# Sixteen chunks of the first feed-forward computed with tokens on the output's partitions

## The chip, the cores and the metric

The kernel runs on one core of a Trainium2 chip. The metric is the device time of one execution in microseconds (us), the median of several runs. The engines are TensorE (PE for its matmuls, PEld for its weight loads), VectorE (DVE), ScalarE (ACT), GpSimd (POOL) and SyncE (SP), which here only issues DMAs. Each engine works through its own queue in order and waits on semaphores for the others.

## What is computed

One layer of a hybrid decoder: 512 tokens (T) of 1024 channels (D), float32 in and out. A SwiGLU feed-forward, a token mixer (recurrent heads beside attention) and a second feed-forward, each between two normalisations. The change touches the first feed-forward, with F = 2816 hidden channels, 22 chunks of 128:

```python
def rms_norm(x, g):
    xf = x.astype(jnp.float32)
    y = xf * lax.rsqrt(jnp.mean(xf * xf, axis=-1, keepdims=True) + RMS_EPS)
    return (y * g.astype(jnp.float32)).astype(x.dtype)

def swiglu(x, w_gu, w_down):
    gate, up = jnp.split(x @ w_gu, 2, axis=-1)
    return (jax.nn.silu(gate) * up) @ w_down
...
        x = x + 0.5 * rms_norm(swiglu(rms_norm(x, ffn1_pre_g[l]), ffn1_w_gu[l], ffn1_w_down[l]), ffn1_post_g[l])
...
        x = x + 0.5 * rms_norm(swiglu(rms_norm(x, ffn2_pre_g[l]), ffn2_w_gu[l], ffn2_w_down[l]), ffn2_post_g[l])
```

Of the mixer only one thing matters here: its recurrence needs a decay factor for each channel, worked out from the parameter lru_lambda alone.

## The kernel before

**Precision.** Every float32 product is done as three matmuls of reduced width: each operand is split into a rounded copy (hi, made by ACT) and the remainder (lo, made by DVE), and hi x hi, hi x lo and lo x hi are summed in PSUM. A weight tile thus costs one ACT copy ("cast") and one DVE subtraction ("low") after it is loaded.

**Seven products for eight.** Most of both feed-forwards uses the Strassen-Winograd scheme: a product of 2 x 2 blocks is made of seven block products ("forms") and sums of blocks. On the weight side the forms p to v need four sums or differences, made in place on the raw tile by DVE before the cast ("pre", run by `combine`: q, r, s and t). On the other side the forms of the normalised input (`nxt.t`) are made once. For the down product the forms of the hidden values are made by `seven_left` and `seven_right` as the values come, with some left in `hid.steps` to be run inside the down product.

**The weight stream.** `Weights` (W) holds the list of raw weight tiles (1 MB each, loaded by SP in two DMAs of 512 KB) and the list of units, that is, of hi and lo pairs made from them, in the order in which TensorE takes them. `W.take(ahead)` keeps the splitting some units ahead; a unit is cast as one ACT instruction of 128x1024, and its low as one DVE instruction of the same size. When the last unit of a raw tile is split, the next raw tile's load is issued (`W.load`), unless something else is owed at that place (`W.owed`). `W.later(n, fn)` runs fn at the n-th take from now. All instructions go out in the program's order, engine by engine (`manual_schedule`): what an engine does next is fixed by that order.

**FFN1.** `GROUPS1` divides the 22 chunks into (0, 4), (4, 8), (8, 12), (12, 16) and (16, 22).
- Group 0 is `classic`: plain products, then a plain down product (matmuls at L421 to L423) whose partial sums go to HBM. At its end `lend` stores the input x to HBM (xT_hbm) to free its buffers.
- Chunks 4 to 21 are made by `quad` (L773), nine times, two chunks at a time. The weights are stationary (128x128), 256 tokens move, and gate and up come out with channels on the partitions: 7 forms of 24 matmuls (L786) into the PSUM banks A, D and B. ACT copies A to B (L805), and ACT and DVE do the sums of the scheme, silu and the product, which gives hidden values with channels on the partitions, as the down product wants them.
- The down product of groups 4, 8 and 12 is `seven_down` with `by_channels` (L1114, matmuls L1122), straight after the group's two quads: 7 forms of 24 matmuls with 256 columns. ACT copies each result to a stage tile, and POOL adds it to the partial sums in HBM (yp_a) by accumulating DMAs (L895).
- The last group (16 to 21) has three quads and a plain down product of 8 output columns, which begins with the earlier sums coming back (`parts`, loaded by POOL's queue); `decay_factor` (L1042, 16 operations on 128x4 and one table of ACT's) runs beside it at its second column.

**FFN2** has quads too, but its `seven_down` is given `by_tokens` (L1624): there the hidden values are stationary, 512 weight columns move, and the sums have tokens on the partitions (matmuls L1630 to L1632, 84 for the seven forms). It begins by turning its input: DVE transposes 32x32 blocks (L1616) and SP puts the pieces to HBM (L1619).

Of the kernel before, what the change touches and what calls it, by code (L numbers as in the profile page):

```python
# [8 lines left out]
F32 = mybir.dt.float32  # L9
# [6 lines left out]
P = 128  # L16
T = 512
# [102 lines left out]
def tile_layer(ctx: ExitStack, tc: tile.TileContext, out: bass.AP, **ins: bass.AP):  # L120
# [94 lines left out]
    def add_quad(w_gu, f, name):  # L215
# [31 lines left out]
        unit(d, "u")  # L247
        unit(b, "v")

    def add_seven_down(wd, f, name):  # L250

        rx, ry = (W.raw(lambda i=i: load_raw([wd[0, (f + k) * P:(f + k + 2) * P, HALF_D[i]] for k in (0, 2)], 2, D, f"{name}{'yx'[i]}d{f}_")) for i in (1, 0))
        first, second = HALF_D
        b11, b21, b12, b22 = (ry, first), (ry, second), (rx, first), (rx, second)

        def of(block):
            return W.tiles[block[0]][:, :, block[1]]

        def unit(block, n, pre=None):
            def cast(raw):  # L260
                hi, lo = w_tiles(2, T, f"{name}d{n}{f}_")
                act.copy(hi, of(block))
                return hi, lo

            def low(raw, hi, lo):
                dve.tensor_sub(lo, of(block), hi.bitcast(F32))

            W.unit(block[0], cast, low, pre)

        def combine(fn, o, x, y):  # L270
            def run():
                assert max(o[0], x[0], y[0]) < W.loaded
                fn(of(o), of(x), of(y))
# [14 lines left out]
        add()  # L288
    GROUPS1 = [(0, 4), (4, 8), (8, 12), (12, 16), (16, 22)]
    for g, (f0, f1) in enumerate(GROUPS1):  # L290
        for f in range(max(f0, 2), f1, 2):
            (add_gate_up if f < CLASSIC1 else add_quad)(w1, f, "a")
        if SEVEN_DOWN1[0] <= f0 < SEVEN_DOWN1[1]:
            add_seven_down(ins["ffn1_w_down"], f0, "a")
# [408 lines left out]
    class Hidden:  # L703
# [66 lines left out]

            self.steps = [lambda: self.low("s2"), last_sum, lambda: self.low("s4"), lambda: self.low("a22")]

        def quad(self, f, last, ahead, seven_down=False):  # L773

            n = f"{self.name}{f}"
            l, r = HALF
# [28 lines left out]
            act.copy(B, A)  # L805
            seven(D, "t3", True)
            act.copy(p7, D)
            seven(A, "t2", False)
            act.copy(u2, A)
            seven(B, "b21", False)  # L810
            W.later(1, act.activation, p1, B, AF.Silu)
            seven(A, "t1", False)
            act.copy(u4, A)
            W.later(1, dve.tensor_add, u4, p7, u4)
            seven(D, "t4", False)
            dve.tensor_add(u2, u2, D)
# [10 lines left out]
            if not seven_down:  # L827
                for j in range(2):
                    self.hs[f + j] = hs[j]

        def classic(self, n, banks, extra, ahead=AHEAD):

# [44 lines left out]
    def seven_down(hid, f, one, part):  # L877


        forms = hid.seven_forms(f)  # L880
# [230 lines left out]
    def in_halves(t):  # L1111
        return t.rearrange("p (a b) -> p a b", a=2)
# [20 lines left out]
        return tiles  # L1133

    parts = [None] * KD
    late = []
    for g, (f0, f1) in enumerate(GROUPS1):
        if SEVEN_DOWN1[0] <= f0 < SEVEN_DOWN1[1]:
# [3 lines left out]
            continue  # L1142
        if f1 == FC:
            W.owed = [lambda: None, lambda: x_tiles.__setitem__(slice(None), give_back())]
        xs = hid.chunks(f0, f1) if g else hid.classic(f1, banks, {})
        if f1 == FC:
            for c in range(KD):
                parts[c] = t2k(f"yp_a{c}")
                pool.dma_start(in_halves(parts[c]), in_hbm[c // 2][:, :, c % 2])  # L1149
        for c in range(KD):  # L1150
            if f1 == FC and c == 0:
                load_gates()
                neg = masks()
            if f1 == FC and c == 1:
                ka, nka = decay_factor()
                preload(AF.Sqrt)
            if f1 == FC and c == 3:
                split_gates()
            if f1 == FC and c >= KD - LATE:
                late.append((c, W.take(0)))  # L1160
                W.fill(3)
                continue
            if c == 0:

                two = [W.take(), W.take()]
                pair_banks = [bank(f"ya{g}{i}") for i in range(2)]
                for k, x in enumerate(xs):
                    for w, b in zip(two, pair_banks):
                        mm3(b, w, k, x, k == 0, k == len(xs) - 1)
            b = pair_banks[c] if c < 2 else product(W.take(), xs, name=f"ya{g}{c}")  # L1170
            if g == 0 and c in (0, 1, 3, 4):
                (n1.sums if c in (0, 3) else n1.lows)(2 + c // 3)
            if g == 0:
                st = t2k("stage")
                act.activation(st, b, AF.Copy, scale=-1.0 if c >= KD // 2 else 1.0)
                pool.dma_start(in_hbm[c // 2][:, :, c % 2], in_halves(st))
                if c == 4:
                    lend(x_tiles)
            else:
                res.chunk(c, b, parts[c])  # L1180

# [565 lines left out]
```

## Time and profile before

| | |
|---|---|
| Time, median of 3 runs | 865.41 us (865.25 to 865.65) |
| The profiled execution's own time | 865.51 us |
| Its span, first to last instruction | 863.8 us |
| TensorE's granted clock in it | 0.998 |
| Busy: PE, PEld | 855.4 us, 797.9 us |
| Busy: DVE, ACT, POOL | 705.0 us, 522.0 us, 219.5 us |
| Moved over DMA | 125.53 MB, mean 145 GB/s |
| First quad of FFN1 starts | 78.64 us |
| First `seven_down` of FFN1 | 118.96 to 139.12 us |

A page of the profile gives busy times of each engine, their share of the span, and the chain of waits: the work that ended last, followed back from the last instruction, at each step to what released it or to the instruction before it on its engine. Lines of groups read "line engine operation output<-input, shape, xcount". Names such as raw_ax, whi_aq or wlo_aq are a raw weight tile of FFN1 and the hi and lo of its unit q; a trailing number is a buffer's. Lines of a timeline read: start in us, duration in us, engine, source line, operation, tiles; "[1.17 <-ACT ...]" at the end is idle time before the instruction and what ended it. Lines of windows read: stretch, its length, busy time (and count) of PE, PEld, DVE, ACT, POOL, granted clock, share of the DMA engines, GB/s.

### The profile page before, as it was taken

The page shows a single profiled execution, that of the slowest core. Times are in us where ns is not written, and L with a number is a line of the kernel's source. Part 1 is how long each engine was busy: PE and PEld are TensorE (multiplying, and loading weights), DVE is VectorE, ACT ScalarE, POOL GpSimd, SP SyncE. Part 2 cuts the span into 40 slices and gives each one's busy share as a digit, 9 for nine tenths or more (in the row PEclk, how much of TensorE's full clock was granted, in tenths as well). Part 3 has the DMA queues.
Part 4 walks back from the last instruction along what each step waited for, and adds up shares of the span by engine and source line. Part 5 has one row for each costly group of instructions (what it writes and reads, how often), then busy time and mean ns, then how long its engine had stood idle before and what let it go on. Part 6 is the DMA issues. An engine that isn't in the chain of part 4 may idle for free.

```text
span 863.8 us, 15057 instructions
## 1 busy us (share of the span) xinstructions
PE 855.4 (99%) x5924; PEld 797.9 (92%) x5924; DVE 705.0 (82%) x972; ACT 522.0 (60%) x874; POOL 219.5 (25%) x236
## 2 busy tenths in 40 slices
PE   9999999999999999999999999999999999999996
PEld 9988999999999998998788899888998998998995
DVE  5979887887897866889989589788789798888856
ACT  6647566566576555466888446444656666657552
POOL 2023004023034024334456055110201302303502
PEclk9999999999999999999999999999999999999999
DMA  7248539639469363221311140266733955938932
GB/s 247 73 159 287 214 100 229 183 93 238 135 121 271 110 211 121 85 88 58 103 46 50 49 146 1 70 173 196 277 92 96 236 154 134 233 98 183 238 118 97
DMA packets 113286, 125.53 MB, mean 145 GB/s; under 512 B 22640, under 2 KB 88512, under 8 KB 112704
## 3 DMA queue, kind: packets, MB, share of 16 engines
q1 hardware_dynamic: 97232, 87.74, 32.1%
q0 software_dynamic: 15840, 36.71, 19.2%
q8 instruction: 46, 0.75, 0.3%
q14 instruction: 24, 0.20, 0.1%
q10 hardware_dynamic: 144, 0.13, 0.0%
HBM read 92.06 MB, written 32.51 MB: 144 GB/s over the span
## 4 chain that ended last, share of the span: by engine, by line
PE 97%; DVE 1%; POOL 1%; ACT 0%; issue 0%; DVEq 0%; POOLq 0%; ACTq 0%
PE aa L786 12%; PE ab L786 11%; PE da L786 6%; PE db L786 5%; PE ba L786 3%; PE yaa L1122 3%; PE bb L786 3%; PE yda L1122 2%; PE ya L422 2%; PE ya L421 2%; PE ya L423 2%; PE a_first L982 1%; PE yb L1606 1%; PE yb L1608 1%; PE yb L1607 1%; PE wo L1561 1%
## 5 line engine op out<-in xcount | busy, mean ns | idle before, releaser
L895 POOL DMA_DIRECT2D yp_b<-stage x42 | 36.3, 1131 | 150.3 <-ACT stage L892 144.4
L895 POOL DMA_DIRECT2D yp_a<-stage x42 | 36.8, 1139 | 146.8 <-ACT stage L892 138.0
L421 PE MATMUL ya<-hha,whi_ad 128*128 128x512 f32 x62 | 24.1, 389 | 0.0
L422 PE MATMUL ya<-hla,whi_ad 128*128 128x512 f32 x62 | 24.1, 389 | 0.0
L423 PE MATMUL ya<-hha,wlo_ad 128*128 128x512 f32 x62 | 24.1, 389 | 0.0
L592 POOL TENSOR_TENSOR acca_r<-acca_r,sq_r 128x512 f32<-128x512 f32 x6 | 10.1, 1679 | 47.2 <-ACT sq_r L452 47.1
L1607 PE MATMUL yb<-wlo_bd,hhb 128*128 128x512 f32 x48 | 18.7, 389 | 0.0
L1606 PE MATMUL yb<-whi_bd,hhb 128*128 128x512 f32 x48 | 18.7, 389 | 0.0
L1608 PE MATMUL yb<-whi_bd,hlb 128*128 128x512 f32 x48 | 18.7, 389 | 0.0
L196 DVE TENSOR_TENSOR wlo_bd<-raw_bd,whi_bd 128x1024 fp32r<-128x1024 f32 x10 | 12.1, 1215 | 5.3 <-ACT whi_bd L191 5.3
L719 POOL TENSOR_TENSOR usb<-usb,gsb 128x512 f32<-128x512 f32 x5 | 7.2, 1440 | 34.1 <-DVE usb L716 22.9
L440 PE MATMUL an<-xh_mx,whi_xl 128*128 128x256 f32 x64 | 15.8, 287 | 0.0
L441 PE MATMUL an<-xh_mx,wlo_xl 128*128 128x256 f32 x64 | 15.5, 283 | 0.0
L1149 POOL DMA_DIRECT2D yp_a<-yp_a x8 | 6.4, 879 | 32.3 <-PE aa L786 26.1
L1706 POOL TENSOR_TENSOR yp_b<-yp_b,grow 128x512 f32<-128x512 f32 x6 | 7.7, 1292 | 26.5 <-ACT ysq L1699 26.5
L421 PE MATMUL gt<-xh_mx,whi_gt 128*128 128x512 f32 x32 | 14.2, 443 | 0.0
L423 PEld LDWEIGHTS ya<-hha,wlo_ad 128*128 128x128 f32 x62 | 11.6, 188 | 2.4
L421 PEld LDWEIGHTS ya<-hha,whi_ad 128*128 128x128 f32 x62 | 11.6, 188 | 2.4
L422 PEld LDWEIGHTS ya<-hla,whi_ad 128*128 128x128 f32 x62 | 11.6, 188 | 2.4
L1654 POOL DMA_DIRECT2D yp_b<-stage x8 | 4.4, 550 | 35.4 <-ACT stage L1653 35.0
L1607 PE MATMUL ybl<-wlo_bd,hhb 128*128 128x512 f32 (+1 forms) x36 | 13.2, 366 | 0.0
L1606 PE MATMUL ybl<-whi_bd,hhb 128*128 128x512 f32 (+1 forms) x36 | 13.2, 366 | 0.0
(1901 smaller groups left out, 3967.5 us busy)
## 6 DMA issues: line engine op xcount, KB each, us to landing
yp_a<-stage POOLq DMA_DIRECT2D x50, 256.0 KB, 7.7
yp_b<-stage POOLq DMA_DIRECT2D x50, 256.0 KB, 8.4
raw_bd<-in_ffn_w_down SPq DMA_DIRECT2D x4, 1024.0 KB, 8.7
xn<-in_x SPq DMA_DIRECT2D x8, 256.0 KB, 4.2
xT_hbm<-xT POOLq DMA_DIRECT2D x2, 1024.0 KB, 5.9
xT<-xT_hbm POOLq DMA_DIRECT2D x2, 1024.0 KB, 13.6
yp_a<-yp_a POOLq DMA_DIRECT2D x8, 256.0 KB, 7.2
raw_q<-in_w_in SPq DMA_DIRECT2D x4, 512.0 KB, 3.7
```

The lines of the kernel that those rows point to most:

```text
L196: low.tensor_sub(two(lo, x), x, two(hi.bitcast(F32), x))
L421: pe.matmul(ps, hi[:, k, :], xh, start=start, stop=False)
L422: pe.matmul(ps, hi[:, k, :], xl, start=False, stop=False)
L423: pe.matmul(ps, lo[:, k, :], xh, start=False, stop=stop)
L440: pe.matmul(ps[:, sl], hi[:, k, :], xh, start=k == 0, stop=False)
L441: pe.matmul(ps[:, sl], lo[:, k, :], xh, start=False, stop=False)
L786: pe.matmul(o, w[:, k, js], x, start=first and i + j + k == 0, stop=k == 3 and i == 2, skip_group_check=True)
L895: pool.dma_start(o, st.rearrange("p (a b) -> p a b", a=2) if len(o.shape) == 3 else st, accum_op=ALU.add)
L1122: pe.matmul(o, a[:, k, ms], x[:, js], start=first and i + k + m % 2 == 0, stop=k == 1 and i == 2, skip_group_check=True)
L1606: pe.matmul(ps, hh[:, blk], hi[:, k, cs], start=start, stop=False)
L1607: pe.matmul(ps, hh[:, blk], lo[:, k, cs], start=False, stop=False)
L1608: pe.matmul(ps, hl_[:, blk], hi[:, k, cs], start=False, stop=stop)
```

## The change

Chunks 4 to 19 of FFN1 are made by a new function `octo`, four times, four chunks at a time; the last two chunks stay a quad. In an octo the input's token blocks are stationary and the weights move, 512 columns at once, so that gate and up come out with tokens on the partitions, as pairs of PSUM banks A, Dd and B; each form takes two weight units and 2 x 12 matmuls.

The result has to be turned for the down product: DVE transposes its 32x32 blocks, SP puts the pieces to HBM (64 KB each, in runs of 128 bytes) and fetches them back with channels on the partitions during the next octo, where the forms for the down product are made by hooks (`beside`). So the down product of a group runs after the octo of the next group: octo 4, octo 8, down 4, octo 12, down 8, octo 16, down 12, quad 20, and then the plain down product of chunks 16 to 21.

Further: in `seven_down` the copies of A to B come ahead of the step of `hid.steps`; the splits of chunks 16 to 19 and `decay_factor` run inside the last quad; the loads of `parts` move from POOL's queue to SP's; the two loads that a `W.later` issued four takes into the first `seven_down` group are issued at the end of group 0.

Instructions in the program: PE's rows go from 5625 to 4985 (672 matmuls fewer), DVE's from 961 to 973, SP's from 199 to 287.

```diff
+    def add_octo(w_gu, f, name):
+        def srcs(half, q):
+            r = half * (D // 2) + q * 2 * P
+            return [w_gu[0, r:r + 2 * P, o + f * P:o + (f + 4) * P] for o in (0, F)]
+
+        rx, ry = ([W.raw(lambda half=half, q=q: load_raw(srcs(half, q), 2, 8 * P, f"{name}{'xy'[half]}{f}{q}_")) for q in range(2)] for half in range(2))
+        gate, up = slice(0, T), slice(T, 2 * T)
...
+        blocks = [((x, gate), (x, up), (y, gate), (y, up)) for x, y in zip(rx, ry)]
+        for i, n in enumerate("pqrstuv"):
+            for a, c, b, d in blocks:
+                unit((a, c, c, b, a, d, b)[i], n, {
+                    "q": combine(dve.tensor_sub, c, a, c), "r": combine(dve.tensor_sub, c, d, c),
+                    "s": combine(dve.tensor_add, a, c, a), "t": combine(dve.tensor_sub, b, b, c)}.get(n))
...
+        if g == 0:
+            for f in range(2, f1, 2):
+                add_gate_up(w1, f, "a")
+        else:
+            add_octo(w1, f0, "a")
+            if g > 1:
+                add_seven_down(ins["ffn1_w_down"], GROUPS1[g - 1][0], "a")
+            if f1 < FC:
+                continue
+            add_quad(w1, f0 + 4, "a")
...
+        def octo(self, f, beside):
...
+            def seven(b, form, first, i):
+                for q in range(2):
+                    hi, lo = W.take()
+                    for tb in range(2):
+                        blk = slice(tb * P, (tb + 1) * P)
+                        for k in range(2):
+                            xh, xl = self.nxt.t[form, 2 * q + k]
+                            for j, (x, w) in enumerate(((xh, hi), (xl, hi), (xh, lo))):
+                                pe.matmul(b[tb], x[:, blk], w[:, k, :], start=first and q + k + j == 0, stop=q + k == 2 and j == 2, skip_group_check=True)
+                    did(i + q / 2)
...
+            def turned(xs, h):
+                zs = pair(wt, f"z{h}")
+                for z, x in zip(zs, xs):
+                    dve.transpose(z, x)
+
+                def put():
+                    for tb, z in enumerate(zs):
+                        for i in range(4):
+                            t0 = (2 * h + tb) * P + 32 * i
+                            o = h_hbm[:, t0:t0 + 32].rearrange("(j a) n -> a j n", a=32)
+                            sync.dma_start(o, z[32 * i:32 * (i + 1)].rearrange("p (j n) -> p j n", n=32))
+
+                W.later(1, put)
...
+            seven(A, "b11", True, 0)
+            each(act.copy, B, A)
+            seven(Dd, "t3", True, 1)
+            each(act.copy, p7, Dd)
+            seven(A, "t2", False, 2)
+            each(act.copy, u2, A)
+            seven(B, "b21", False, 3)
+            W.later(1, each, silu, p1, B)
+            seven(A, "t1", False, 4)
+            each(act.copy, u4, A)
+            W.later(1, each, add, u4, p7)
+            seven(Dd, "t4", False, 5)
+            each(add, u2, Dd)
+            each(mul, u2, p1)
+            W.later(1, turned, u2, 0)
+            seven(A, "b22", False, 6)
+            each(silu, g1, A)
+            W.later(1, each, mul, g1, u4)
+            W.later(1, turned, g1, 1)
+            return h_hbm
+
+        def seven_forms_of(self, f, h_hbm):
+            x = {}
+
+            def fetch():
+                for s in range(2):
+                    for h in range(2):
+                        x[s, h] = t2k(f"hx{self.name}{f}{s}{h}")
+                        sync.dma_start(x[s, h].rearrange("p (j n) -> p j n", j=2), h_hbm[2 * s * P:2 * (s + 1) * P, HALF[h]].rearrange("(j p) n -> p j n", p=P))
...
+            return {2: [fetch], 3.5: [begin], 4.5: [lambda: self.seven_right(f, x[0, 1], 0)], 5: [lambda: self.seven_left(f, x[1, 0], 1)],
+                    5.5: [lambda: self.seven_right(f, x[1, 1], 1)], 6: [lambda: self.steps.pop(0)()]}
...
+        def last_chunks(self, f, h_hbm, extra):
+
+            self.fetched(f, h_hbm)
+            todo = list(range(f, f + 4))
+            self.quad(f + 4, True, AHEAD, beside=lambda i: (extra.get(i, lambda: None)(), self.split(todo.pop(0))))
+            return [self.hs.pop(c) for c in range(f, f + 6)]
...
             one(banks, W.take(), forms[form], form in ("a11", "s3", "s4"))
+            if form == "a11":
+                for i in range(2):
+                    act.copy(B[i], A[i])
             if hid.steps:
                 hid.steps.pop(0)()
-            for i in range(2):
-                if form == "a11":
-                    act.copy(B[i], A[i])
-                    continue
...
-        if SEVEN_DOWN1[0] <= f0 < SEVEN_DOWN1[1]:
-            if g == 1:
-                W.later(4, W.load, 2)
-            seven_down(hid, f0, by_channels, lambda half, dh, i: in_hbm[2 * dh + i][:, half])
-            continue
...
+            h_hbm[f0] = hid.octo(f0, hid.seven_forms_of(before, h_hbm[before]) if g > 1 else {})
+            if g > 1:
+                seven_down(hid, before, by_channels, lambda half, dh, i: in_hbm[2 * dh + i][:, half], hid.forms)
...
+            xs = hid.last_chunks(f0, h_hbm[f0], {3: lambda: decay.append(decay_factor())})
...
-                pool.dma_start(in_halves(parts[c]), in_hbm[c // 2][:, :, c % 2])
+                sync.dma_start(in_halves(parts[c]), in_hbm[c // 2][:, :, c % 2])
...
                 if c == 4:
                     lend(x_tiles)
+                    W.load(2)
```

More of the change, by code (lines that the diff above doesn't have):

```diff
@@ L248, in add_quad, with of, unit, cast @@
         unit(b, "v")
+    def add_octo(w_gu, f, name):
[4 more added lines that the diff above has]
+        gate, up = slice(0, T), slice(T, 2 * T)
+        def of(block):
+            return W.tiles[block[0]][:, :, block[1]]
+        def unit(block, n, pre=None):
+            def cast(raw):
+                hi, lo = w_tiles(2, T, f"{name}{n}{f}_")
+                act.copy(hi, of(block))
+                return hi, lo
+            def low(raw, hi, lo):
+                dve.tensor_sub(lo, of(block), hi.bitcast(F32))
+            W.unit(block[0], cast, low, pre)
+        def combine(fn, o, x, y):
+            def run():
+                assert max(o[0], x[0], y[0]) < W.loaded
+                fn(of(o), of(x), of(y))
+            return run
+        blocks = [((x, gate), (x, up), (y, gate), (y, up)) for x, y in zip(rx, ry)]
[4 more added lines that the diff above has]
+                    "s": combine(dve.tensor_add, a, c, a), "t": combine(dve.tensor_sub, b, b, c)}.get(n))
     def add_seven_down(wd, f, name):
@@ L771, in seven_right, with quad @@
             self.steps = [lambda: self.low("s2"), last_sum, lambda: self.low("s4"), lambda: self.low("a22")]
-        def quad(self, f, last, ahead, seven_down=False):
+        def quad(self, f, last, ahead, seven_down=False, beside=lambda i: None):
             n = f"{self.name}{f}"
@@ L831, in classic, with fetched @@
+        def fetched(self, f, h_hbm):
+            for c in range(f, f + 4):
+                x = t2k(f"hx{self.name}{c}")
+                sync.dma_start(x, h_hbm[(c - f) * P:(c - f + 1) * P])
+                self.u[c] = x
         def classic(self, n, banks, extra, ahead=AHEAD):
```

48 lines of the change are left out of this document (36 added, 12 removed).

## The prediction

> **What bounds the kernel now.** I read the page's totals and the shares of the chain of waits first, then the chain in order of time around the first feed-forward, then the engines' busy time by stage, then the timelines of VectorE (DVE), ScalarE (ACT) and the queue of SyncE (SP).
>
> ```profile
> span 863.8 us, 15057 instructions
> PE 855.4 (99%) x5924; PEld 797.9 (92%) x5924; DVE 705.0 (82%) x972; ACT 522.0 (60%) x874; POOL 219.5 (25%) x236
> ...
> PE 97%; DVE 1%; POOL 1%; ACT 0%; issue 0%; DVEq 0%; POOLq 0%; ACTq 0%
> ...
> PE warm L969 <- POOL ident masks.py:199: 1.4, 1, 1.4
> PE po L1440 <- POOL pa L1427: 0.2, 1, 0.2
> ```
>
> TensorE is busy for 99% of the span and makes 97% of the chain; over the whole run it waits for others only 1.6 us (the two rows of waits). So time falls by what TensorE no longer does, and rises by each new wait of TensorE. Nothing saved on another engine counts. But DVE, busy 82%, is the next bound.
>
> ```profile
> 78.19 0.23 PE ya L422
> 78.42 0.23 PE ya L423
> 78.64 2.87 PE aa L786 x24
> 81.52 2.88 PE da L786 x24
> ...
> 118.96 2.88 PE yaa L1122 x24
> ```
>
> The chain gives the price of a matmul. The quads (L786) and FFN1's down product (L1122), with 256 columns moving, run 24 in 2.88 us, 120.0 ns each. The plain down product just before (L422, L423) has 512 columns and goes at 0.23 us each.
>
> ```profile
> 118.96:139.12 20.16, 20.16 (x170) 20.16 (x170) 18.15 (x20) 15.59 (x24) 7.06 (x8) 1.00 0.69 166
> 657.02:676.09 19.07, 19.07 (x87) 15.78 (x86) 17.06 (x20) 14.49 (x23) 6.84 (x8) 1.00 0.68 164
> 139.12:179.44 40.32, 40.32 (x338) 40.32 (x338) 32.55 (x33) 23.04 (x31) 5.27 (x6) 1.00 0.68 166
> ```
>
> Columns: stretch, its length, busy time (and count) of PE, PEld, DVE, ACT and POOL, granted clock, DMA share, GB/s. The first two rows are one and the same set of seven products (84 blocks of 128x128 by 512 columns): in the first feed-forward's down product as 168 matmuls of 256 columns, in the second's as 84 of 512. TensorE is full in both at clock 1.00: 20.16 us against 19.07, that is 227.0 ns for a matmul of 512. The weight load fills the first row (20.16 of 20.16) and leaves room in the second (15.78 of 19.07).
>
> **The change part by part.** *1. The products.* Eight quads (chunks 4 to 19, two chunks each) become four octos of 7 x 24 matmuls of 512 columns. Eight sets of 168 x 120.0 ns give 161.3 us, eight of 84 x 227.0 ns 152.5 us: 8 x (20.16 - 19.07) = **8.7 us less**. An octo then takes 168 x 227.0 ns = 38.1 us where two quads took 40.32 (third row); one half-form (12 matmuls) takes 2.72.
>
> [...] The rows here show 240.0 against 227.0 ns, 13 ns per pair, and I go by them.
>
> *2. Start of the first octo.* An octo takes four raw weight tiles of 1 MB instead of two for each quad, and uses all four by its third form.
>
> ```profile
> 79.28 1.52 SPq L156 DMA_DIRECT2D raw_ay__1063<-in_ffn_w_gu  x2
> ...
> raw_ay__860<-in_ffn_w_gu SPq DMA_DIRECT2D x2, 512.0 KB, 4.7
> ...
> 79.00:82.00 3.00, 3.00 (x27) 3.00 (x27) 2.97 (x4) 2.45 (x5) 1.04 (x2) 1.00 1.01 375
> 82.00:87.00 5.00, 5.00 (x44) 5.00 (x44) 5.00 (x5) 3.83 (x5) 0.69 (x1) 1.00 0.96 309
> ...
> 90.80 1.22 DVE L240 TENSOR_TENSOR raw_ax__1002<-raw_ay__1063,raw_ax__1002 128x1024 f32<-128x1024 f32 x1
> ...
> 82.73 0.59 ACT L805 COPY ba<-aa 128x512 f32<-128x512 f32 x1
> 184.48 1.05 ACT L262 CAST whi_adv__2254<-raw_ayd__1807 128x1024 fp32r<-128x1024 f32 x1
> ```
>
> The second y tile takes the place of raw_ay__1063 in SP's queue: issued at 79.28 for 1.5 us, 4.7 us to land as a load of this kind does, so not before 85.5; and at 90.80, when DVE reads it now without waiting, it is there. The DMA engines are full then (1.01 and 0.96), so I take 87. Now nobody needs it before 90.80; the octo needs it for the fourth of its weight units that are differenced (r1). Behind r1's cast in ACT's queue stand the next cast and the copies of the first form's sum from bank A to bank B, and TensorE's fifth half-form writes A: due at 78.64 + 4 x 2.72 = 89.5. From 87: difference on DVE 1.1, two casts 1.05 each, copy 0.59: 90.8. **Wait 1.2 us**; with 85.5 none, with 90.8 five.
>
> *3. The three transitions octo to down product.* Down products of group n now run after the octo of group n+1, their left operands fetched back from HBM and turned into forms during that octo. Each octo also has four DVE transposes that the quads lacked (the result has tokens on the partitions).
>
> ```profile
> 150.01 1.22 DVE L235 TENSOR_TENSOR wlo_aq__1841<-raw_ax__1475,whi_aq__1840 128x1024 fp32r<-128x1024 f32 x1 [1.17 <-ACT whi_aq__1840 L231]
> 155.96 0.68 DVE L113 TENSOR_TENSOR u4a<-p7a,u4a 128x512 f32<-128x512 f32 x1
> 156.56 0.68 DVE L816 TENSOR_TENSOR u2a<-u2a,da 128x512 f32<-128x512 f32 x1
> ...
> 166.87 1.22 DVE L273 TENSOR_TENSOR raw_axd__1746<-raw_axd__1746 128x1024 f32<-128x1024 f32 x1
> 168.01 1.22 DVE L266 TENSOR_TENSOR wlo_adp__2046<-raw_ayd__1807,whi_adp__2045 128x1024 fp32r<-128x1024 f32 x1
> ...
> L1616 DVE STREAM_TRANSPOSE z<-xT x8: 659/682/705, 556.3 to 587.2; 128x512 f32<-128x512 f32 x8
> ```
>
> Start to start DVE takes 1.14 us for 1024 elements (166.87 to 168.01) and 0.60 for 512. Per cycle of octo and down product it has 32.55 + 18.15 = 50.7 us now; with four transposes of 0.6 it has 53.1 in 38.1 + 20.16 = 58.3 us, 91%. On top come waits for casts (the 1.17 in the first row): two units each at q and r, 4 x 1.17 = 4.7. That is 57.8 of 58.3: just enough over a cycle, but not at each point. In program order DVE has, from TensorE's end of the eighth half-form (octo + 21.8, which frees a weight buffer), 9 operations of 1024 and 14 of 512 and a wait of about 1 before the weights of the down product's third form can be cast: 21.8 + 9 x 1.14 + 14 x 0.61 + 1 = 41.6, plus the fifth form's difference 1.1 = 42.7; then ACT's cast 1.05 and copy 0.59 give 44.3. TensorE's third form of the down product writes that copy's bank and is due at 38.1 + 2 x 2.88 = 43.9. **Wait 0.5 us, three times: 1.5.** With the full recorded durations (1.22 and 0.68) it is 2.3 each; with one wait less, none. B's copy now stands ahead of the forms' step on ACT, which keeps it early.
>
> *4. SP's queue and the traffic through HBM.* Each octo issues 16 puts of 64 KB (pieces of 128 bytes), and four fetches of 256 KB.
>
> ```profile
> 574.35 4.11 SPq L1619 DMA_DIRECT2D x_hbm<-z  x8
> ...
> L1619 SPq DMA_DIRECT2D x_hbm<-z x32: 302/490/513, 557.1 to 591.1; - x32
> ...
> 560.00:562.00 2.00, 2.00 (x11) 1.65 (x10) 1.51 (x4) 1.57 (x2) 0.00 (x0) 1.00 0.69 119
> 570.00:572.00 2.00, 2.00 (x11) 1.65 (x10) 2.00 (x5) 0.34 (x1) 0.00 (x0) 1.00 0.91 349
> ...
> yp_a<-stage POOLq DMA_DIRECT2D x50, 256.0 KB, 7.7
> ```
>
> The same puts exist at the start of the second feed-forward: eight hold SP for 4.11 us, so 16 take 8.2 us of its queue per octo. Behind the second eight stands the next octo's fourth weight load; the second result's transposes end some 7 us into the down product in DVE's order, so the load is issued 11.4 us into it (7.3 and 4.1). Counting DVE's operations on from there, DVE wants it at about 22.6; TensorE, which has five weight pairs in hand, from about 28. In those 16.6 us a load of 1 MB that lands in 4.7 alone has room, also among the down product's sums into HBM (7.7 us each of 256 KB): 0, with the bound in the rivals. The fetches wait in SP's queue only for puts that were issued 20 us or more before: 0.
>
> [...]
>
> *5. What is moved into the last quad.* It gets four splits (copy on ACT, remainder 0.6 on DVE) and the 16 small operations of the decay factor.
>
> ```profile
> L1055 DVE TENSOR_SCALAR s<-z x1: 170/170/170, 331.0 to 331.0; 128x4 f32<-128x4 f32 x1
> L1053 ACT ACTIVATE z<-nabs x1: 205/205/205, 330.8 to 330.8; 128x4 f32<-128x4 f32 x1
> ```
>
> 4 x 0.6 + 16 x 0.17 = 5.1 us on DVE, whose idle time in a quad is (40.32 - 32.55)/2 = 3.9; the rest pushes weight operations that have about that much lead. Taken at 0, up to 0.9. They stood beside plain products before, so nothing of TensorE's comes free there. The parts' loads leave POOL's queue for SP's, some 10 us ahead of their use: 0; so is the earlier load in group 0.
>
> *Sum:* 8.7 - 1.2 - 1.5 = 6.0. The profiled execution took 865.51 (span 863.8 and 1.7 around it); 865.5 - 6.0 = 859.5. The median of the runs lies 0.1 lower: **859.4 us**.
>
> **The rivals.** *No waits at all.* The load lands by 85.5 and DVE keeps its lead: 865.4 - 8.7 = 856.7. For it: TensorE waits for nobody now though DVE is at 90% in the down product (18.15 of 20.16). Against it: 57.8 of 58.3.
>
> *Slower: DVE becomes the bound of the cycle.* If it also waits for casts at s and t, as at q and r, that is 8 x 1.17 = 9.4 us per octo: 53.1 + 9.4 = 62.5 for 58.3, so 4.2 late in each of three cycles. 856.7 + 1.2 + 12.6 = 870.5. It decides from (8.7 - 1.2)/3 = 2.5 us late per cycle, 7.7 us of waits. For it: each interleaved unit pair shares its sources, so one unit's difference feeds the cast of the same unit. Against it: at s and t the low parts of units before stand between.
>
> *Slower: the fourth load comes late.* If the load and the neighbouring loads (2 MB) share with as much of the down product's sums at 166 GB/s (first window), they take 25 us, 8.7 beyond the 16.6; half of it, 4.3, at three transitions gives 859.4 + 12.9 = 872.3. It too decides from 2 us per transition. Against it: puts of the second half are small (0.5 MB).
>
> [...]
>
> **How the numbers follow.** Forecast 0.55, no waits 0.16, DVE as the bound 0.15, late load 0.08, no saving 0.03, and 0.03 for something else, either way. The forecast's own range takes waits of 0.3 to 7 us: 857 to 863.5. A measurement of this kernel can tell about 0.2% (1.7 us) from no change: 863.7 to 867.1 is the same. With the forecast's upper bounds together (5.2 + 6.9 + 0.9) it would reach 869.7, which is slower; half of 0.06 for it. Faster: 0.51 + 0.16 + 0.04 of the rest and mild forms = 0.72; same: 0.06; slower: 0.22. The range goes from just below the case without waits, 856.0, to 869.0, where the mild forms of the slower cases lie; about 0.2 is left out.
>
> **What would show each step.** The octo's matmuls must stand at 227 ns and an octo at 38.1 us plus waits. The waits of TensorE should name ACT's copy to bank B at the first octo's fifth half-form (1.2) and at each down product's third form (0.5). DVE should be busy about 53 us per cycle, its transposes at 0.68. The fourth load must land within 16 us of its issue. The last quad should show no gap. Waits over 8.7 us in sum, whoever is waited for, prove the forecast wrong, and so does a matmul of 512 columns above 235 ns.

## The result and the profile after

| | before | after |
|---|---|---|
| Time, median of 20 runs each | 865.41 us (865.08 to 866.00) | 868.85 us (864.81 to 873.27) |
| Ratio | | 1.0041, 95% interval 1.0028 to 1.0053 |
| The profiled execution's own time | 865.51 us | 873.27 us |
| Its span | 863.8 us | 871.5 us |

The changed kernel is slower by 0.4%, where 0.7% faster was forecast; and its runs spread over 8.5 us, those of before over 0.9. The profiled execution is the slowest of its runs, so the bill below is that of the slowest run, not of the median. In the comparisons further down one execution of e1 took 1700 us, one of e3 1192 us and one of the kernel before 1402 us; the ratios leave these three out.

The page's totals and the shares of the chain, and TensorE's waits over the whole run (us in total, times, longest), of the kernel after:

```profile
span 871.5 us, 13882 instructions
PE 852.4 (98%) x5252; PEld 764.8 (88%) x5252; DVE 710.0 (81%) x984; ACT 520.9 (60%) x871; POOL 211.6 (24%) x228
...
PE 78%; DVE 8%; DMA 7%; issue 3%; ACT 3%; POOL 1%; SPq 0%; DVEq 0%; ACTq 0%
...
PE aa L896 <- ACT ba L901: 4.9, 2, 4.5
PE ya L463 <- ACT hha L835: 3.5, 1, 3.5
PE warm L1116 <- POOL ident masks.py:199: 1.4, 1, 1.4
PE yba L1269 <- ACT yba L1034: 0.9, 3, 0.3
PE aa L828 <- ACT u4a L858: 0.6, 1, 0.6
```

The profile counts 5252 matmuls where it counted 5924, 672 fewer. TensorE is busy 3.0 us less, not 8.7, and it has some 10 us of waits that weren't there. DMA, no part of the chain before, is 7% of it. Two waits count: 4.5 us inside an octo (L896) and 3.5 us at the first plain down product (L463). The chain in order of time says where:

```profile
101.29 5.44 PE aa L896 x24
...
171.69 16.30 DMA raw_ay__1727<-in_ffn_w_gu
188.02 1.24 DVE raw_ax__1499 L277
189.47 0.77 issue
190.23 1.04 ACT whi_as__1942 L266
191.27 0.49 ACT ba L901
191.81 7.84 PE aa L896 x24
...
303.19 9.50 DMA hxa<-h_a
312.71 0.63 ACT hha L766
313.35 14.81 DMA raw_ad__3288<-in_ffn_w_down
```

Undisturbed, 24 matmuls of 512 columns take 5.44 us, 226.7 ns each. *First loss:* the third octo's fourth weight load takes 16.3 us from its issue; then follow DVE's difference, ACT's cast and the copy to bank B, the very steps that the prediction had written out for the first octo, and TensorE. Its next 24 matmuls take 7.84 us. *Second loss:* at the end of the last quad, where the fetch of h (hxa) takes 9.5 us, ACT's cast waits for it, and the weight load raw_ad__3288, next in the chain, takes another 14.8 us.

The 2.4 us by which 7.84 exceeds 5.44 are a slower clock. Windows of TensorE after the two waits (the columns as before; granted clock third from the end):

```profile
190.00:194.80 4.80, 2.99 (x7) 2.41 (x8) 4.44 (x4) 4.80 (x8) 0.00 (x0) 0.50 1.12 236
194.80:199.60 4.80, 4.80 (x19) 3.82 (x19) 4.80 (x6) 2.96 (x4) 0.00 (x0) 0.84 0.77 179
...
331.38:336.10 4.72, 4.72 (x13) 3.55 (x14) 3.50 (x6) 2.35 (x4) 0.00 (x0) 0.65 0.91 264
336.10:342.00 5.90, 5.90 (x27) 4.84 (x27) 3.11 (x4) 3.75 (x7) 1.43 (x2) 0.99 0.96 323
```

The clock is granted at half for 4.5 us behind the first wait and for 3.4 us behind the second (windows of 0.5 us). From 331.38 to 336.45 13 matmuls took 5.07 us where 13 x 0.227 = 2.95: 2.1 us more. So the bill of this execution is: -8.7 for the products, +4.9 and +3.5 for the two waits (0.4 of the first at the first octo), +0.9 at the three down products, +1.2 for three small ones, +2.4 and +2.1 for the clock: +6.3, of the 7.7 by which the span grew. Of the 1.4 left, 0.8 lie in the three down products: from its first matmul to the next stage's first each takes 20.72 us where it took 20.16, 0.56 more, of which the recorded wait is 0.3. The other 0.6 are not traced.

### The profile page after: what moved, and what is told of

It is laid out like the page before. It is cut to its first block, busy times and chain, and to the rows that moved or that the text cites. A ratio compares the mean times of both kernels' runs of the same rounds, so it can differ in the third digit from the quotient of the medians.

```text
span 871.5 us, 13882 instructions
## 1 busy us (share of the span) xinstructions
PE 852.4 (98%) x5252; PEld 764.8 (88%) x5252; DVE 710.0 (81%) x984; ACT 520.9 (60%) x871; POOL 211.6 (24%) x228
## 4 chain that ended last, share of the span: by engine, by line
PE 78%; DVE 8%; DMA 7%; issue 3%; ACT 3%; POOL 1%; SPq 0%; DVEq 0%; ACTq 0%
PE ab L828 11%; PE aa L896 5%; PE db L828 5%; PE bb L828 3%; PE ba L896 2%; PE da L896 2%; DMA raw_ay__1727<-in_ffn_w_gu 2%; DMA raw_ad__3288<-in_ffn_w_down 2%; PE a_first L1129 1%; PE yb L1760 1%; PE yb L1759 1%; PE yb L1758 1%; PE ya L463 1%; PE ya L464 1%; PE ya L465 1%
## 5 line engine op out<-in xcount | busy, mean ns | idle before, releaser
L463 PE MATMUL ya<-hha,whi_ad 128*128 128x512 f32 x62 | 24.9, 401 | 3.5 <-ACT hha L835 3.5
L463 PEld LDWEIGHTS ya<-hha,whi_ad 128*128 128x128 f32 x62 | 12.1, 195 | 6.4 <-ACT hha L835 3.9
L463 PE MATMUL gt<-xh_mx,whi_gt 128*128 128x512 f32 x32 | 14.2, 444 | 0.0
L1760 PE MATMUL ybl<-whi_bd,hlb 128*128 128x512 f32 (+1 forms) x36 | 13.2, 365 | 0.0
```

The lines of the kernel that those rows point to most:

```text
L463: pe.matmul(ps, hi[:, k, :], xh, start=start, stop=False)
L1760: pe.matmul(ps, hl_[:, blk], hi[:, k, cs], start=False, stop=stop)
```

## The experiments

Two theories. *Traffic:* transfers that the change issues or moves meet on the DMA engines, weights land late, TensorE waits and then runs at half clock. *VectorE:* DVE is so full that the waits would come whatever the DMAs do. What SP issues around the first loss (start, duration on SP), and POOL's first sums into HBM there:

```profile
163.07 7.02 SPq L913 DMA_DIRECT2D h_a<-z1a  x8
170.19 4.51 SPq L156 DMA_DIRECT2D raw_ay__1727<-in_ffn_w_gu  x2
...
166.60 3.64 POOL L1042 DMA_DIRECT2D yp_a<-stage  x4 [81.26 <-ACT stage L1039]
```

The eight puts ahead of the load take 7.0 us, against 4.1 in the profile of before, and the sums begin in the middle of them.

**e1: the load ahead of the puts.**

```diff
-                W.later(1, put)
+                W.later(4 if h else 1, put)
```

> The changed kernel with the puts of the second half of an octo's result issued three takes later, so that the next octo's fourth weight load stands ahead of them in SP's queue. Traffic theory: in the changed kernel this load (raw_ay__1727) was issued at 170.19, right behind 7.0 us of puts, landed 16.3 us later and held TensorE for 4.5 us at the third octo, after which TensorE ran at half speed for some 5 us (2.4 us more). Here the load must be issued several us earlier, and that wait and the half-speed stretch must be gone: about 865 us (median of the changed kernel 868.85). The stall of 3.5 us at the last down product stays. VectorE theory (DVE is the bound of a cycle whatever the DMAs do): the wait at the third octo stays, 869 us.

Measured: 863.55 us, ratio 0.9981 (0.9971 to 0.9991). SP's timeline and TensorE's largest new waits:

```profile
161.62 0.93 SPq L156 DMA_DIRECT2D raw_ay__1719<-in_ffn_w_gu  x2
162.70 12.68 SPq L913 DMA_DIRECT2D h_a<-z1a  x8
...
PE aa L828 <- ACT u2a L852: 1.8, 1, 1.8
PE yba L1269 <- ACT yba L1034: 1.0, 3, 0.3
PE ya L463 <- ACT hha L835: 0.5, 1, 0.5
```

The load goes out at 161.6, no octo waits over 0.3 us, and 5.3 us are gone, where about 4 were expected: the order in SP's queue decides the first loss. The 5.3 are not that loss alone, since the wait at the first plain down product is small here too (0.5). The puts now take 12.7 us, and no wait of TensorE names them. A wait of 1.8 us stands in the last quad: there the first split's cast waits for the fetched h, and the copy to u2 that TensorE needs stands behind it on ACT.

**e4: the same puts in whole rows of 2 KB.** The output's blocks then lie elsewhere than they should.

```diff
-                            o = h_hbm[:, t0:t0 + 32].rearrange("(j a) n -> a j n", a=32)
-                            sync.dma_start(o, z[32 * i:32 * (i + 1)].rearrange("p (j n) -> p j n", n=32))
+                            sync.dma_start(h_hbm[t0:t0 + 32], z[32 * i:32 * (i + 1)])
```

> The changed kernel with the octo's result put to HBM in whole rows of 2 KB in place of pieces of 128 bytes: the same 16 puts of 64 KB each at the same places in the queue (the output is then not the layer's, since the blocks of 32 lie elsewhere). If the small pieces are what makes the traffic slow: the second half's puts hold SP for about 4 us in place of 7, the fourth load lands early enough, and the wait at the third octo goes: about 865 us. If the sums into HBM by POOL's queue alone make the load late: it lands as late as now, 868 to 869 us. At the last down product nothing changes by either.

Measured: 864.81 us, ratio 0.9991 (0.9981 to 1.0000).

```profile
163.32 4.42 SPq L912 DMA_DIRECT2D h_a<-z1a  x8
167.84 0.93 SPq L156 DMA_DIRECT2D raw_ay__1727<-in_ffn_w_gu  x2
...
PE ya L463 <- ACT hha L835: 2.4, 1, 2.4
PE aa L896 <- ACT ba L901: 0.6, 1, 0.6
```

With rows the puts take 4.4 us, the load is issued 2.3 us earlier, as the sums only begin, and the octo's wait is gone; the one at the last down product stays. So the first loss needs the small pieces. What they meet, by the DMA queues of the kernel after, first with the puts alone (156 to 162), then beside the sums (168 to 176; packets, MB, share of the 16 engines; q1 is SP's, q0 POOL's):

```profile
q1 hardware_dynamic: 4224, 0.52, 57.2%
...
q0 software_dynamic: 521, 0.96, 72.1%
q1 hardware_dynamic: 2064, 0.26, 30.7%
```

Alone, the puts move their 0.52 MB in some 4.5 of the 6 us. Beside the sums SP's queue gets 31% of the engines and moves 0.26 MB in 8 us, 32 GB/s. The profile counts 2064 packets of SP's queue there (126 bytes each) against 521 of POOL's (1.8 KB each); how the engines share their time between the two it doesn't show. It shows that the queue with the small packets moves few bytes beside the other (0.26 MB against 0.96), and that the weight load behind them in the same queue comes late, 16.3 us after its issue.

**e5: no transposes.** The puts take the unturned tiles; 16 operations of DVE are left out.

```diff
-                zs = pair(wt, f"z{h}")
-                for z, x in zip(zs, xs):
-                    dve.transpose(z, x)
+                zs = xs
```

> The changed kernel without the octos' transposes on DVE (16 of 0.6 us are left out; the puts take the unturned tiles, so the output is not the layer's). VectorE theory: the cycle of octo and down product has 2.4 us less of DVE, the waits at the third octo and at the down products shrink by about as much: 2 to 5 us off the changed kernel's 868.85. Traffic theory: the puts start some 1 to 2 us earlier at most, the fourth load stays behind them; at the last quad nothing changes; within 2 us of the changed kernel.

Measured: 859.00 us, ratio 0.9927 (0.9912 to 0.9942), nearly 10 us off the changed kernel, which neither theory had expected. Two rows tell how:

```profile
160.39 5.24 SPq L911 DMA_DIRECT2D h_a<-g1a  x8
165.73 1.38 SPq L156 DMA_DIRECT2D raw_ay__1711<-in_ffn_w_gu  x2
```

The puts start 2.7 us earlier than in the kernel after and end before most of the sums begin. The wait at the first plain down product is smaller too, 1.6 us for 3.5, which is part of the 10 us; why is not traced. DVE's lag doesn't hold TensorE by itself (e1 has all the transposes and no octo wait above 0.3); it decides whether the puts run into the sums. The first loss is a race between them, and order (e1), size of pieces (e4) and DVE's lag (e5) each turn it. With puts and load as in the change, the wait at the third octo was 4.5 us in the profiled execution of the kernel after, but 0.5 in that of e2 and 1.0 in that of e6, below, where the load went out at 169.1 and 169.5 in place of 170.2.

**e2 and e3: the return of x.** At the end of FFN1 the 2 MB of x come back to SBUF on POOL's queue. In the kernel before this stood at 265.56, in the kernel after at 312.25, since the change moved the place where `W.owed` is set; the load raw_ad__3288 was issued 1.1 us later. e2 has

```diff
-                W.owed = [lambda: None, lambda: x_tiles.__setitem__(slice(None), give_back())]
+                W.owed = [W.load, W.load, lambda: None, lambda: x_tiles.__setitem__(slice(None), give_back())]
```

and e3 both this and e1's edit.

> The changed kernel with the return of the input x from HBM (xT<-xT_hbm, 2 MB on POOL's queue) owed two raw tiles later, behind the last down product's third and fourth weight loads instead of ahead of them. Traffic theory: in the changed kernel the return starts at 312.3 (265.6 before the change) and the weight load raw_ad__3288, issued at 313.35, lands 14.8 us later; the cast that waits for it holds ACT 7.8 us and TensorE 3.5 us, plus 2.1 us at half speed. Here raw_ad__3288 must be issued near 298 and TensorE's wait at the first plain down product must be gone: about 864 us, some 5 less than the changed kernel; the wait at the third octo stays. VectorE or ACT theory (the splits and the decay factor moved into the last quad are too much for it): the wait stays at 3 us or more, 869 us.

> Both edits of the two runs before together. Traffic theory: both large waits go, what is left of TensorE's new waits is 2 to 3 us in sum (0.4 at the first octo, 0.3 at each down product, 0.8 in the last quad): 865.4 - 8.7 + 2.5 = 859 us, faster than before the change. If the gains of the two runs don't add, or another load becomes late in their place, 862 to 866. VectorE theory: 868 us.

Measured: e2 866.23 us (ratio 1.0002, 0.9983 to 1.0022), e3 862.83 us (0.9979, 0.9959 to 0.9999). In e2 the wait stays:

```profile
300.88 0.42 SPq L156 DMA_DIRECT2D raw_ad__3132<-in_ffn_w_down  x1
...
321.60 0.83 ACT L191 CAST whi_ad<-raw_ad__3132 128x768 fp32r<-128x768 f32 x1 [7.52 <-DMA raw_ad__3132<-in_ffn_w_down]
...
PE ya L463 <- ACT hha L835: 3.3, 1, 3.3
```

The load is issued 12 us earlier (some 6 of them because this execution waited only 0.5 us at the third octo) and then takes 20.7 us; x's first half still starts only 6.7 us behind it. So the order of the two alone isn't the cause. In e3's profiled execution the wait at the first plain down product is gone, but one of 2.6 us stands in the last quad, for the fetched h as in e1, and e3 adds only 0.7 us to e1.

**e6: no sums of the third down product.** Its 14 accumulating DMAs are left out, and with them its share of the result.

```diff
+                    if hid.name != "a" or f != 12:
                         pool.dma_start(o, st.rearrange("p (a b) -> p a b", a=2) if len(o.shape) == 3 else st, accum_op=ALU.add)
```

> The changed kernel without the 14 accumulating DMAs (256 KB each) of the third down product, the one that now runs just ahead of the last quad (its partial sums are then left out of the result). If it is these sums, moved from 40 us ahead of the last down product to its threshold, that starve the loads there: the return of x starts some 10 us earlier, raw_ad__3288 lands in under 8 us in place of 14.8, and TensorE's wait at the first plain down product (3.5 and 2.1 at half speed) goes; about 864. If the return of x and the loads of the parts suffice for it, the wait stays above 2 us. The wait at the third octo stays by both.

Measured: 863.65 us (0.9995, 0.9975 to 1.0016), with no wait at the first plain down product at all: the load, issued at 304.73, is there by 312.9. DMA share (last column but one) from 294 on, in the kernels before, after, and e6:

```profile
294.00:317.68 23.68, 23.68 (x200) 23.68 (x199) 15.85 (x19) 13.51 (x22) 5.43 (x9) 1.00 0.46 154
...
294.00:330.00 36.00, 33.10 (x251) 31.39 (x249) 23.51 (x40) 22.07 (x34) 13.29 (x18) 1.00 1.09 279
...
294.00:320.00 26.00, 26.00 (x202) 25.28 (x201) 21.87 (x42) 21.21 (x34) 3.51 (x6) 1.00 0.54 181
```

Before, the last quad was the quiet stretch in which the last weights came in. "One group later" has put the third group's sums into it, beside the return of x, the fetch of h and the parts, and the engines are full. But e6 doesn't take the sums alone out of this stretch: without them x comes back earlier, half of it from 287 on and half from 301 on, ahead of the load. e6's median is no better than e1's. Three of its ten runs lie at 868.1 to 870.7, as if the first loss struck in them; none of them was profiled.

**e7 and e8: the splits later.** e7 is e1 with the last quad's splits two at its third and two at its fourth hook; e8 adds e2's edit.

```diff
-beside=lambda i: (extra.get(i, lambda: None)(), self.split(todo.pop(0)))
+beside=lambda i: (extra.get(i, lambda: None)(), [self.split(todo.pop(0)) for _ in range(2 if i > 2 else 0)])
```

> Late puts as in e1 (863.55) and the last quad's four splits two at its third and two at its fourth hook in place of one at each of four. In e1 the first split's cast waited 4.87 us on ACT for the fetched h, and behind it the copy to u2 held TensorE 1.8 us, with a half-speed stretch after it. Theory (ACT's queue order passes the late fetch on): that wait goes, and raw_ad__3288 is issued earlier, since DVE no longer waits for the same cast: 860 to 861. Rival (the splits merely move their delay to the end of the quad): the wait at the first plain down product takes its place, 863.

> e7 with the return of x owed two raw tiles later, as in e2 and e3. If what is left at the last down product is the order of its weight loads and the return of x: 857 to 859, all waits but those of 0.3 at the down products gone. If the DMA engines are simply full there (share 1.0 from 294 on in e2, where the load took 20 us with the return behind it), it gives nothing over e7.

Measured: 866.16 (1.0006, 0.9996 to 1.0015) and 865.51 us (1.0001, 0.9991 to 1.0011). The wait in the quad goes, and one of 5.2 (e7) and 3.6 us (e8) at the first plain down product takes its place: TensorE is earlier there, and the load lands no earlier. That was the rival's form of it, and dearer than the rival said (863). In e7 the load is issued at 301.04 and ACT can use it at 321.4; x starts between:

```profile
302.17 2.12 POOL L1279 DMA_DIRECT2D xT<-xT_hbm  x2
...
321.40 0.83 ACT L191 CAST whi_ad<-raw_ad__3284 128x768 fp32r<-128x768 f32 x1 [10.25 <-DMA raw_ad__3284<-in_ffn_w_down]
```

**e9 and e14: the return of x behind three loads.** e7 with `W.owed = [W.load, W.load, W.load, lambda: None, ...]`; e14 is the same kernel again, with more rounds.

> e7 (late puts, late splits: 866.16, a wait of 5.2 us at the first plain down product because its third weight load, issued at 301, landed 20 us later) with the return of x owed three raw tiles later, behind the first load of the mixer's weights. If the 2 MB of x that come back at 303 to 320 starve that load: it lands by 311 to 314, the wait goes, 859 to 861. If the sums of the third down product and the loads of the parts are enough for it (as e8 hints, where the return was two tiles later and the load still took 19 us): the wait stays above 2 us, 864.

> The kernel of e9 again. If its first four runs were typical, the median is 859.5 to 860.5, clearly faster than before the change; if the spread of 859.0 to 863.4 is that of a race between its transfers, the median lies between, 860 to 862.

Measured: e9 859.88 us (0.9933, 0.9916 to 0.9950), e14 859.50 us (0.9937, 0.9925 to 0.9948). x comes back from 311 on, where it came from 302 on in e7; the load is issued at 301.1, as in e7. The profile of e14, the same two rows and TensorE's waits (beside one of 1.4 us at the very start that the kernel before has too):

```profile
311.25 0.59 POOL L1279 DMA_DIRECT2D xT<-xT_hbm  x1
...
315.48 0.84 ACT L191 CAST whi_ad<-raw_ad__3132 128x768 fp32r<-128x768 f32 x1 [3.04 <-DMA raw_ad__3132<-in_ffn_w_down]
...
PE yba L1269 <- ACT yba L1034: 0.9, 3, 0.3
PE aa L896 <- ACT ba L901: 0.3, 1, 0.3
```

The two large waits are gone, with nothing left out of the change or the layer, and this version beats both kernels. ACT still waits 3.0 us for the load, but TensorE doesn't; e9's profiled execution, at 863.41 its slowest, had 6.5 us there and 2.1 on TensorE.

**e12 and e13: the mixer's load held back too, and x where it was.** e12 is e9 with the mixer's first weight load held back to x's place; x itself stays there (311.4, against 311.3 in e14), and the parts' loads move up to 303.6. e13 is e7 with `W.owed` set ahead of the last octo.

> Late puts and late splits as in e7, with the return of x and the mixer's first weight load both owed until the last down product's third raw tile is used up, so that only the sums, the fetched h and the parts share the DMA engines with its third weight load. If x takes the share that the load lacks: it lands by 312, the wait at the first plain down product is under 1 us, 858.5 to 860. If the sums and the parts alone starve it: the wait stays above 2 us, 862 to 864. A new risk: x or the mixer's weights come late at the boundary behind (a wait of TensorE after 345).

> e7 with the return of x put back where it was before the change: owed by the first two raw tiles that are used up in the last octo, some 45 us earlier. If its move is the cause of the wait at the last down product: gone or under 1 us. But two raw tiles fewer are then ahead of the last octo, which needs four: its weight loads are issued later, and a wait at the last octo's third form can take its place. 859 if only the first holds, 864 to 870 if the second does.

Measured: e12 860.37 us (0.9954, 0.9930 to 0.9978), five of seven runs at 858.3 to 861.2 and two at 866; e13 877.15 us (1.0129, 1.0114 to 1.0144). e13's waits:

```profile
PE aa L828 <- ACT u2a L852: 9.4, 1, 9.4
PE yba L1269 <- ACT yba L1034: 5.6, 3, 5.0
```

Four raw tiles for an octo leave no room to hand two of the five buffers back early: in e13 x takes two of them from 245 on, and the chain leads both waits back to weight loads. So x's return is shown to matter: with the load issued at the same time, x 9 us later (and a load of the mixer's weights ahead of it) lets ACT use the load at 315.5 in e14's profiled execution and at 318.7 in e9's, in place of 321.4 in e7's, and most runs of e9, e14 and e12 are near 859. The loads of the parts alone don't starve it, since in e12 they stand right behind it. That the sums starve it together with x fits e6, but no run takes the sums alone away. What sets the runs of 866 in e12 isn't settled.

**e10 and e11: the additions u4 + p7 on POOL.** e10 is e9 with the puts where the change has them, e11 is e9 itself, both with

```diff
-            W.later(1, each, add, u4, p7)
+            W.later(1, each, lambda o, x: pool.tensor_add(o, o, x), u4, p7)
```

> The changed kernel with the octos' eight additions u4 + p7 on POOL in place of DVE (1.2 us of DVE less per octo, nothing left out), late splits and the return of x three raw tiles later; the puts stand where the change has them. Theory (DVE's lag at the end of an octo makes the puts run into the sums, as e5's 859.0 without transposes says): the puts start 1 to 2 us earlier, the second half's puts take 4 to 5 us in place of 7 to 13, the fourth load lands in time, all octo waits under 1 us: 860. If 1.2 us isn't enough, the wait at the third octo stays: 864 to 868.

> e9 and the additions on POOL together. Theory: fourth loads early by their place in the queue, puts early by DVE's lighter load, return of x out of the way: no wait over 1 us left, 857.5 to 859.5, clearly faster than before the change. Rival: the end of the third group's traffic stays what bounds it, as in e7 and e8: 863 to 866.

Measured: 865.92 (1.0010, 0.9999 to 1.0021) and 865.43 us (0.9997, 0.9975 to 1.0019). e11, which differs from e9 by the additions alone, is 5.6 us worse; in e10 the third octo waits again, 2.2 us. Beside POOL's additions DVE lost what it had saved (two of 0.6 us) and more (1.1 and 1.0 us in the rows below). One such place in e11, and TensorE's wait:

```profile
144.13 3.56 POOL L936 TENSOR_TENSOR u4a<-u4a,p7a 128x512 f32<-128x512 f32 x2 [35.77 <-DMA raw_ax__1499<-in_ffn_w_gu]
...
144.21 2.33 DVE L303 TENSOR_TENSOR wlo_adp__1504<-raw_ayd__1421,whi_adp__1503 128x1024 fp32r<-128x1024 f32 x1
146.57 1.66 DVE L780 TENSOR_TENSOR hla<-hxa,hha 128x512 fp32r<-128x512 f32 x1
...
PE yba L1269 <- ACT yba L1034: 3.8, 3, 1.3
```

The 1024 operation takes 2.33 us and the 512 one 1.66; in e7's profile, where DVE does the additions itself, the same two take 1.22 and 0.69. The wait at the three down products grows from 0.3 to 1.3 us each. e11's profiled execution, 862.57, is one of its fastest; what made the others slower, up to 871, is not traced.

## Why the prediction was wrong, step by step

*1. The products: right.* 226.7 ns against 227.0 foreseen. The chance of 0.03 for no saving stood on a price of two halves over one whole that no run shows; the runs showed 240.0 ns for two matmuls of 256 columns (before) and 226.7 for one of 512 (after), 13.3 ns more. *2. First octo: right in kind, 0.4 us for 1.2.* The load landed at 86.2, where 87 was taken. *3. The transitions: right in place and chain, and nearly in size.* The waits for bank B's copy came at each third form, with 0.3 us recorded for 0.5; the three down products together got 1.7 us longer, where 1.5 was forecast.

*4. The queue: this is the step that failed.* It said that the fourth load "has room, also among the down product's sums", and took 0. It priced the puts at 4.1 us as they run alone, and the load at 4.7; beside the sums they took 7.0 and 16.3. The room that it saw was right: it let TensorE do without the load until about 28 us into the down product. That product began at 155.5; the load was issued 14.7 us into it, not 11.4, and was there at 32.5, so 4.5 late, which is the wait measured. In the median e1 gave 5.3 us back. The rival "the fourth load comes late" had the kind of loss right, a load that shares the DMA engines with the sums. Its price, 4.3 us, was half of a sharing that it worked out without the puts, so its nearness to 4.5 is luck; and it put it at three transitions, where the profiled execution shows it at one. Its argument against, that the puts are small, was the error: small pieces were dear beside the sums (7.0 us, for 4.4 in rows, e4).

*5. The last quad: failed by what was left out.* It counted the splits and the decay factor on DVE, and found the room there; but not that "one group later" also takes the third group's sums and the return of x later, onto the loads of the last down product. Before, DMA was at 0.46 there; the step never looked at that window. It took the whole step at 0, up to 0.9. Cost in the profiled execution: 3.5 us, and 0.6 and 0.2 in the quad, where ACT's casts for the splits wait for the fetch.

*What no step had:* the two large waits cost more than themselves. In the profiled execution the half clock added 4.5 us to their 8.0.

*The rivals.* "No waits" would have been 856.7; e12's and e14's fastest runs reach 858.3 and 858.4. "DVE becomes the bound" is refuted as it stood (e1 and e14 have all DVE work and no such wait), though its lag sets off the race (e5).

The sum holds where the traffic is out of the way: e14's span is 857.7, 6.1 us below before's 863.8, where 6.0 was forecast, and its median 859.5 where 859.4 was. That it is so near is in part luck. By stages, e14's octos took 153.0 us (forecast 153.7 with the first wait), its three down products 1.7 us more than before (forecast 1.5) and its last quad 0.1 more; that makes 6.5 us less, and 0.4 us are lost elsewhere and not traced.

## What to carry to other kernels

When a change delays a stage, list what moves with it on every queue (sums, returns of lent buffers, loads), and lay each over the DMA share of the windows in which it lands; a quiet stretch on the DMA engines can be what the next stage's loads live on, as the one at 0.46 was here. A put in small pieces must be priced beside the traffic that it will meet (7.0 us here), not as it runs alone (4.1), and loads that something waits for belong ahead of it in the queue. A spread of the runs that grows, here from 0.9 to 8.5 us, is a hint to look for transfers in a race.

## What the runs showed of the hardware

**Half clock behind waits of 1.8 us and more.** In the profiled executions, TensorE's waits of up to 1.6 us (the longest of these in e5, at the first plain down product) were followed by no slow stretch of even 1 us. Each of eleven waits of 1.8 us and more, in those of the kernel after (two), e1, e3, e4, e7 to e10 and e13 (two), was followed by some 3.4 to 6.0 us at about half speed, which cost some 1.7 to 3 us: from one matmul of 512 columns to the next 0.43 us for 0.23, and with 256 columns 0.21 for 0.12. Read in windows of 0.5 us, the half clock of the kernel after stood from 189.5 to 196.3 at the first wait (187.3 to 191.8), 6.8 us, and from 332.8 to 336.2 at the second (327.9 to 331.4), 3.4 us: it began 2.2 us after the first had begun, inside it, and 4.9 us after the second had, 1.4 us behind its end. The shortest, in e1, a window before, at and behind it:

```profile
303.00:307.00 4.00, 2.24 (x20) 2.03 (x18) 1.24 (x2) 1.83 (x3) 2.38 (x4) 1.00 1.09 250
307.00:310.50 3.50, 3.50 (x17) 3.50 (x18) 2.87 (x8) 3.42 (x6) 0.00 (x0) 0.55 1.11 229
310.60:314.00 3.40, 3.40 (x30) 3.40 (x30) 3.06 (x13) 3.37 (x6) 2.65 (x5) 0.98 1.06 347
```

No run made waits of set lengths, so what a wait of a given length does to the clock is not settled.

**DVE beside POOL's additions.** While POOL added u4 and p7 in e11 (3.56 us from 144.13), a subtraction of DVE's of 1024 elements took 2.33 us and one of 512 took 1.66; the same two took 1.22 and 0.69 in e7, where DVE does these additions itself. Both read two operands, as POOL's additions do; DVE's other operations beside POOL's were not traced.
